# Side work of the tensor engine gathered at parts four and eight of each slot, with the turns priced in the planner (hybrid decoder step, one core)

## The chip, the cores and the metric

The kernel runs on one core of a Trainium2 chip. The metric is the device time of one launch in microseconds (us), on that core; the median of some runs is quoted, and one further execution was recorded by the hardware profiler. A core has a tensor engine (PE, with its weight loads as PEld), a vector engine (DVE), a scalar engine (ACT), GpSimd (POOL), and a queue (SP) that here issues all the transfers between memory and the on-chip buffers.

## The reference

One layer of a decoder is computed for 512 prompt rows and, beside them, for 8 sample rows (one new token in each of 8 sequences with 4096 past tokens, whose keys and values lie in pages of 128 tokens). Everything is fp32.

```python
u = rms_norm(h, g_norm)
z = u @ w_in                                   # 2048 -> 7168
q, k, v, gate_a, cu, gate_c = jnp.split(z, IN_SPLITS, axis=-1)
q, k = partial_rope(q, pos), partial_rope(k, pos)          # 8 heads, two maps of 64 each
o = attn_fn(q, k, v, lam)                      # softmax(map 0) - lam * softmax(map 1), times v
o_att = (rms_norm(o, g_subln) * (1.0 - lam_init)) * jax.nn.silu(gate_a)
g = ca * jax.nn.sigmoid(cb)                    # cu split in two
c = causal_dwconv(hist, w_dw, b_dw)            # 31 taps
o_conv = (jax.nn.silu(layer_norm(c, g_cln, b_cln)) @ w_pw) * jax.nn.silu(gate_c)
h = h + jnp.concatenate([o_att, o_conv], axis=-1) @ w_out
h = h + jax.nn.sigmoid(rms_norm(h, g_ple) @ w_pg) * (p_l @ w_ple)
y = rms_norm(h, g_final)
```

For the prompt, attention is causal over the 512 rows. For the samples it runs over the cache: 8 sequences of 32 key pages and 32 value pages, each page 128 x 1024 numbers (0.524 MB). New keys, values and convolution rows are returned too.

## The kernel before

**Dense products.** All products of the 512 prompt rows with weights are done in 196 slots. A slot loads weights of 256 x 512 (tile `raw`, three buffers); ACT rounds each half to `hi` and POOL takes the rest, `lo = raw - hi`; the activations stand as `aht` and `alt`. Each product is three matmuls of 512 columns into one of four accumulators `acc` (one for each 128 rows of the prompt): hi by high, hi by low, lo by high. A slot has eight parts (four accumulators by two halves of the weights), each part being these three matmuls; the 16 slots of the last two groups of `w_pg` have four parts. There are 4512 such matmuls in the program, and "dense product 3840" below is the 3840th of them. `run_slot` emits the parts and calls `hook(n)` after part n (n from 0).

**Side work.** Everything else that the tensor engine does is put between the parts: transposes through a bank `misc`, the prompt's attention (`att_unit`: scores, transposes of the weights `tmp`, products with `dt`, the transposed result `o`), the statistics of the sample rows, and the decode. The decode has, for each sequence, 32 key pages (tile `kt`, multiplied by the query on DVE, then summed by head on DVE or, sixteen pieces a page, on ACT), a softmax, and 32 value pages (`vt`, or `kt` when the keys are through) that PE multiplies by the weights `aw` into the bank `pers`: four matmuls a page, one on each strip of 32 columns of the array. The sample rows' products with weights are likewise four matmuls on four strips (`pers<-raw,usT`). When the last value page is done, `v_end` and `sample_tail` make the samples' attention output `oS`, multiply it by `w_out` (16 pages of weights through the same two rings, `misc<-kt,mST`), add it to the residual (`xs`), and only then is `usT`, the samples' input to `w_pg`, there; 32 pages of `w_pg` follow (`misc<-kt,usT`). `samp`, in the second slot of the last group, waits for that `usT`.

**What sets the order.** The program is a fixed order for each engine, written when the kernel is built. A class `Planner` keeps a clock for each engine and adds a cost for each instruction it is told of. Each side task is a generator that yields conditions: `on(eng, tiles)` is true when the planned clock of that engine is not ahead of PE's by more than 0.5 us and the tiles are planned to be ready (0.5 us before PE's clock, if PE itself is to read them). `hook` pumps the weight loads and the two rings (five `kt`, two `vt` buffers), resumes each task whose condition holds, and then `decode_tick` gives key products to DVE as long as DVE's planned clock is at most 0.4 us ahead of PE's, and value pages to PE: two or more at any part, a single one only at n = 7. `settle(cond)` is a wait in the plan: it calls `hook` again and again and moves PE's clock until the condition holds, and no dense product is emitted meanwhile. All engines work through their own order and wait for each other by semaphores. All profile rows stand at line 209, the helper that records each instruction, so they are told apart by tiles.

Of the kernel before, what the change touches and what calls it, by code (L numbers as in the profile page):

```python
# [60 lines left out]
class Planner:  # L61
# [2 lines left out]

    FAR = dict(PE=200, V=135, A=130, G=120, Q=70)
    NEAR = dict(PE=0, V=125, A=125, G=60, Q=0)

    def __init__(self):
        self.t = dict(PE=0.0, V=0.0, A=0.0, G=0.0, Q=0.0, D=0.0)
        self.hist = {}  # L70
        self.late = dict(V=[], G=[])

    @staticmethod
    def is_ap(x):
# [86 lines left out]
    def put(self, eng, fn, args, kw, cost=None):  # L161
        outs, ins = [], []
        for i, x in enumerate(args):
            if self.is_ap(x):
                (outs if i == 0 else ins).append(x)
        for k, x in kw.items():
            if self.is_ap(x):
                (outs if k in ("out", "accum_out") else ins).append(x)
        start = self.t[eng]
        dram = lambda x: x.name.startswith(("in_", "out_"))  # L170
        if eng == "Q":
            far = [x for x in outs + ins if dram(x)]
            outs = [x for x in outs if not dram(x)]
            ins = [x for x in ins if not dram(x)]
        start = max([start] + [self.ready(x, True, eng) for x in outs] + [self.ready(x, False, eng) for x in ins])
        if eng == "Q":
            self.t["Q"] = start + 450
            nb = 4
            for d in (outs + ins + far)[0].shape:
                nb *= d  # L180
            self.t["D"] = max(self.t["D"], start + 1100) + nb / 345.0
            end = self.t["D"] + 865
        else:
            c = self.cost(eng, fn, outs, ins, kw) if cost is None else cost
            port = eng in "VG" and self.holds(eng, fn, ins)
            if port:
                start = self.port(eng, start, c)
                self.push(eng, start, c)
            end = start + c
            self.t[eng] = end  # L190
        notes = [self.note(x, True, end, eng) for x in outs] + [self.note(x, False, end, eng) for x in ins]
        if eng in "VG":
            ops = self.late[eng]
            ops.append(dict(at=start, cost=c, port=port, notes=notes))
            del ops[:-16]
# [19 lines left out]
def hymba_step(ctx, tc, x_prompt, x_sample, p_prompt, p_sample, cache_k, cache_v, state_conv, page_table,  # L215
# [4 lines left out]
    plan = Planner()  # L220
    clk = plan.t
# [47 lines left out]
    def on(eng, *aps):  # L269

        back = -500.0 if eng == "PE" else 500.0
        return lambda: (eng == "PE" or clk[eng] <= clk["PE"] + back) and all(plan.ready(x) <= clk["PE"] + back for x in aps)

    def small(n, name, bufs=1):
        return sm.tile([128, n], F32, tag=name, name=name, bufs=bufs)
# [59 lines left out]
    def spawn(gen, now=False, rank=1):  # L335

        tasks.insert(sum(t[2] <= rank for t in tasks), [next(gen) if now else None, gen, rank])

    def hook(n=7):
        wpump()  # L340
        kring.pump()
        vring.pump()
        if cur[0] < 168:
            split_ahead()
        for t in list(tasks):
            for _ in range(3):
                if t[0] is not None and not t[0]():
                    break
                try:
                    t[0] = next(t[1])  # L350
                except StopIteration:
                    tasks.remove(t)
                    break
                if t[0] is None:
                    break
        if cur[0] >= 168:
            split_ahead()
        decode_tick(n)
# [232 lines left out]
    def v_pages(tiled):  # L591

        n = v_here()
        if n < (1 if tiled else 2):
            return
        s = dec["iv"] // NPAGE
        vper[0] = s
        for k in range(n):
            ring = kring if kring.here(VALS) and (not vring.here(VALS) or kring.tiles[0][2] < vring.tiles[0][2]) else vring
            vt, idx = ring.get()  # L600
            for cg in range(4):
                mm(pers[32 * cg:32 * cg + 8, 0:256], aw[s % 2][:, idx % NPAGE, :], vt[:, cg * 256:(cg + 1) * 256],
                   start=False, stop=True, cost=20 if cg else 370 + (0 if k or tiled else 150))
            ring.done(vt)
            dec["iv"] += 1
            vdone[s] += 1
        if vdone[s] == NPAGE:
            spawn(v_end(s), rank=0)
# [236 lines left out]
    def samp(i):  # L845
# [20 lines left out]
        for ii in mem:  # L866
            q = slots[ii]
            for kk in range(2):
                k = q["ks"][kk][0]
                for g in range(4):  # L870
                    mm(pers[32 * g:32 * g + 8, col:col + 128], s["sample"][:, k, :],
                       raws[ii][:, kk, g * 128:(g + 1) * 128], start=False, stop=(q["last"] and kk == 1),
                       cost=20 if g else 214 + 10)
        for ii in mem:
            release(ii)
        if s["last"]:
# [513 lines left out]
    def sample_tail():  # L1390
# [24 lines left out]
        def tail_pass(first, last, lhs):  # L1415
# [3 lines left out]
            for _ in range(last - first):  # L1419
# [5 lines left out]
                for a in range(nn):  # L1425
                    for g in range(4):
                        mm(ps[32 * g:32 * g + 8, (n + a) * 128:(n + a + 1) * 128], lhs[:, k, :],
                           wt[:, a * 512 + g * 128:a * 512 + (g + 1) * 128], start=False, stop=True,
                           cost=20 if g else 214 + 10)
                ring.done(wt)  # L1430
            tail_state["ps"] = ps
        yield from tail_pass(0, 16, mST)
# [42 lines left out]
    with tc.manual_schedule():  # L1475
# [126 lines left out]
        def early_q():  # L1602
# [5 lines left out]
            for n in range(16):  # L1608
# [3 lines left out]
                for a in range(2):  # L1612
                    for g in range(4):
                        mm(pers[32 * g:32 * g + 8, a * 128:(a + 1) * 128], usT[:, k, :],
                           wt[:, a * 512 + g * 128:a * 512 + (g + 1) * 128], start=False, stop=True,
                           cost=20 if g else 214 + 10)
                ring.done(wt)
            yield on("A", pers[:, 0:256])
            qs = yield from take("tmp")
# [103 lines left out]
```

## Time and profile before

| what | value |
|---|---|
| median of 3 runs | 1570.15 us (1565.2 to 1571.04) |
| the profiled execution, its own time | 1576.48 us |
| its span, first to last instruction | 1574.6 us |
| PE / DVE / ACT / POOL busy | 1482.9 / 1100.8 / 811.7 / 622.9 us |
| moved by DMA | 424.40 MB, mean 270 GB/s |
| longest waits of PE, 60 to 1490 us | for `lo` 14.6 us in 26 times, for `pers` 5.0 us in 8 |

The page gives, for each engine, the time in which it was busy; matmuls are pipelined, and the start of one to the start of the next tells better what one costs than its own duration. The view of stretches (windows) gives the same for pieces of the span, with the granted clock of PE (1.00 is 2.4 GHz, 0.50 is 1.2 GHz) and the rate of the transfers. The view in order of time (timeline) lists instructions with their start, their duration, and in brackets the idle time of the engine before them and what ended it.

### The profile page before, as it was taken

The numbers are of one execution on the slowest core, as the hardware profiler recorded it, in microseconds if no ns is written. First come the engines' busy times: TensorE is split into PE (matmuls) and PEld (weight loads), VectorE is DVE, ScalarE is ACT, GpSimd is POOL, SyncE is SP. The second block draws the span as 40 slices with busy tenths as digits, with TensorE's granted clock in tenths as the row PEclk, the third lists the DMA queues.
The fourth block names the chain that finished last, engine by engine and source line by source line (L and its number), as shares of the span: only waits on it lengthen the run. The fifth ranks groups of instructions, "written<-read, shape, count | busy, mean of one in ns | idle before, by whom it ended". The sixth has DMA issues, their size and how long they took to land.

```text
span 1574.6 us, 32145 instructions
## 1 busy us (share of the span) xinstructions
PE 1482.9 (94%) x10448; PEld 1039.5 (66%) x10448; DVE 1100.8 (70%) x1636; ACT 811.7 (52%) x3810; POOL 622.9 (40%) x471
## 2 busy tenths in 40 slices
PE   5899999999999999999999999999999999999786
PEld 4676767666667766677777667766767777665453
DVE  5168987788798978888888868878867888301201
ACT  4156666556655645562445567665655765414202
POOL 5144534323333433344443454434423365425312
PEclk8999999999999999999999999999999999999877
DMA  7648779767887876543358687599878799899997
GB/s 287 233 169 294 273 257 358 275 228 256 320 282 279 296 251 207 188 135 124 126 168 295 228 307 254 187 350 340 299 258 332 275 327 382 306 328 337 395 320 255
DMA packets 148921, 424.40 MB, mean 270 GB/s; under 512 B 14192, under 2 KB 16226, under 8 KB 148480
## 3 DMA queue, kind: packets, MB, share of 16 engines
q1 hardware_dynamic: 148752, 422.35, 75.7%
q8 instruction: 82, 1.34, 0.3%
q14 instruction: 87, 0.71, 0.1%
HBM read 413.62 MB, written 9.63 MB: 269 GB/s over the span
## 4 chain that ended last, share of the span: by engine, by line
PE 75%; DMA 11%; DVE 5%; POOL 3%; issue 3%; ACT 2%; SPq 1%; POOLq 0%; ACTq 0%; DVEq 0%
PE acc L209 57%; PE pers L209 11%; PE misc L209 7%; DMA raw<-in_w_in_dram 4%; POOL lo L209 2%; DVE kt L209 1%; DMA raw<-in_w_out_dram 1%; DMA kt<-in_w_out_dram 1%; DMA raw<-in_w_pg_dram 1%; DVE bt L209 1%; DMA vt<-in_cache_v_dram 1%; DVE sc L209 1%; DMA kt<-in_w_pg_dram 1%; DMA kt<-in_cache_v_dram 0%; ACT hi L209 0%
## 5 line engine op out<-in xcount | busy, mean ns | idle before, releaser
L209 POOL TENSOR_TENSOR lo<-raw,hi 128x512 fp32r<-128x512 f32 x392 | 557.7, 1435 | 829.7 <-ACT hi L209 775.1
L209 ACT CAST hi<-raw 128x512 fp32r<-128x512 f32 x392 | 236.6, 618 | 437.1 <-PE acc L209 218.1
L209 DVE TENSOR_TENSOR kt<-kt,qb 128x1024 f32<-128x1024 f32 x256 | 363.9, 1436 | 41.1 <-DMA kt<-in_cache_k_dram 36.7
L209 PE MATMUL acc<-hi,aht 128*128 128x512 f32 x896 | 377.8, 422 | 7.8 <-ACT hi L209 7.5
L209 PE MATMUL acc<-lo,aht 128*128 128x512 f32 x896 | 360.9, 403 | 17.5 <-POOL lo L209 17.5
L209 PE MATMUL acc<-hi,alt 128*128 128x512 f32 x896 | 357.9, 399 | 0.2 <-DVE alt L209 0.2
L209 ACT ACTIVATE kt<-kt 128x64 f32<-128x64 f32 x1392 | 336.1, 244 | 25.2 <-DVE kt L209 25.2
L209 ACT ACTIVATION_READ_ACCUMULATOR kt<-kt 128x1 f32 x1392 | 262.2, 188 | 0.0
L209 PE MATMUL acc<-aht,hi 128*128 128x512 f32 x576 | 245.6, 426 | 3.9 <-DVE bt L209 3.4
L209 PE MATMUL acc<-aht,lo 128*128 128x512 f32 x576 | 228.8, 397 | 4.5 <-POOL lo L209 4.4
L209 PEld LDWEIGHTS acc<-hi,aht 128*128 128x128 f32 x896 | 170.2, 190 | 92.8 <-issue 32.4
L209 PE MATMUL acc<-alt,hi 128*128 128x512 f32 x576 | 227.5, 395 | 0.0
L209 PEld LDWEIGHTS acc<-lo,aht 128*128 128x128 f32 x896 | 170.7, 190 | 68.4 <-POOL lo L209 28.3
L209 DVE TENSOR_REDUCE sc<-kt 128x16 f32<-128x1024 f32 x169 | 203.4, 1210 | 1.3
L209 PEld LDWEIGHTS acc<-hi,alt 128*128 128x128 f32 x896 | 171.2, 191 | 33.3 <-DVE alt L209 0.7
L209 DVE SCALAR_TENSOR_TENSOR misc<-ft,wdwT,misc 128x512 f32<-128x512 f32 x240 | 180.3, 751 | 6.2
L209 PEld LDWEIGHTS acc<-aht,hi 128*128 128x128 f32 x576 | 108.5, 188 | 65.0 <-issue 34.3
L209 PEld LDWEIGHTS acc<-aht,lo 128*128 128x128 f32 x576 | 108.2, 188 | 34.8 <-POOL lo L209 9.2
L209 PEld LDWEIGHTS acc<-alt,hi 128*128 128x128 f32 x576 | 108.6, 189 | 18.0 <-issue 0.2
L209 PE MATMUL pers<-vt,aw 128*8 128x256 f32 x1624 | 113.4, 380 | 6.3 <-DVE pers L209 5.0
L209 DVE SCALAR_TENSOR_TENSOR acc<-acc,ct 128x512 f32<-128x512 f32 x16 | 11.2, 699 | 128.9 <-ACT acc L209 128.9
L209 PEld LDWEIGHTS pers<-vt,aw 128*8 128x8 f32 x1624 | 31.8, 88 | 62.9 <-issue 32.5
(259 smaller groups left out, 1283.2 us busy)
## 6 DMA issues: line engine op xcount, KB each, us to landing
kt<-in_cache_k_dram SPq DMA_DIRECT2D x256, 512.0 KB
vt<-in_cache_v_dram SPq DMA_DIRECT2D x203, 512.0 KB
raw<-in_w_in_dram SPq DMA_DIRECT2D x112, 512.0 KB
kt<-in_cache_v_dram SPq DMA_DIRECT2D x53, 512.0 KB
raw<-in_w_pg_dram SPq DMA_DIRECT2D x40, 512.0 KB
raw<-in_w_out_dram SPq DMA_DIRECT2D x32, 512.0 KB
kt<-in_w_in_dram SPq DMA_DIRECT2D x12, 512.0 KB
kt<-in_w_out_dram SPq DMA_DIRECT2D x12, 512.0 KB
```

The source lines that it names most:

```text
L209: real(*args, **kw)
```

## The change

The planner gets a constant `TURN = 92` (ns): whenever PE goes from a dense product to anything else, or back, 92 ns are added to the planned cost. The other planned costs of strip matmuls are set anew: a value page 410 + 3 x 7 ns for its four matmuls (before: 370 + 3 x 20, and 150 more for the first page of a run at another part than the last), a set of four sample matmuls 205 + 3 x 7 (before 224 + 3 x 20). And a condition is added: tasks that wait with `on("PE", ...)`, and value pages, may go on only when `turn()` holds, that is, after part 4 and part 8 of a slot (n = 3 and 7), or while no dense product runs, or in a `settle`. Tasks that wait for a free bank alone (`take`), or for a page in a ring, are not held back. No instruction is computed otherwise; the order and the place of the side work change, and with the planned clock the place of the work on the other engines.

```diff
     FAR = dict(PE=200, V=135, A=130, G=120, Q=70)
     NEAR = dict(PE=0, V=125, A=125, G=60, Q=0)
+    TURN = 92
...
             c = self.cost(eng, fn, outs, ins, kw) if cost is None else cost
+            if eng == "PE":
+
+                dense = outs[0].name.startswith("acc")
+                c += self.TURN if dense != self.dense else 0
+                self.dense = dense
...
-        return lambda: (eng == "PE" or clk[eng] <= clk["PE"] + back) and all(plan.ready(x) <= clk["PE"] + back for x in aps)
+        return lambda: (eng != "PE" or turn()) and (eng == "PE" or clk[eng] <= clk["PE"] + back) and all(plan.ready(x) <= clk["PE"] + back for x in aps)
...
+    step = [0]
+
+    def turn():
+
+        return not main_on[0] or step[0] % TURNS == TURNS - 1
+
+    TURNS = 4
+
     def hook(n=7):
+        step[0] = n
         wpump()
...
         n = v_here()
-        if n < (1 if tiled else 2):
+        if n < (1 if tiled else 2) or not turn():
             return
...
-                   start=False, stop=True, cost=20 if cg else 370 + (0 if k or tiled else 150))
+                   start=False, stop=True, cost=7 if cg else 410)
...
-                       cost=20 if g else 214 + 10)
+                       cost=7 if g else 205)
```

The last pair of lines stands at three more places (`samp`, `tail_pass`, `early_q`).

In the built program both kernels have the same 7697 matmuls. What changes is where they stand. On PE, in the first half of the prompt's attention, these rows follow each other before (`misc<-ft,bt` are scores, `misc<-cst,tmp` and `misc<-cst,o` transposes, `misc<-dt,tmp` products with the values, `pers<-vt,aw` value pages of the decode, four matmuls each):

```order
L209 MATMUL misc<-cst,o 128x128
L209 MATMUL acc<-aht,hi 128x512
L209 MATMUL acc<-alt,hi 128x512
L209 MATMUL acc<-aht,lo 128x512
L209 MATMUL misc<-cst,tmp 128x128
L209 MATMUL pers<-vt,aw_121 8x256 x8
L209 MATMUL acc<-aht,hi 128x512
L209 MATMUL acc<-alt,hi 128x512
L209 MATMUL acc<-aht,lo 128x512
L209 MATMUL misc<-dt,tmp 128x128
L209 MATMUL misc<-ft,bt 128x384 x2
```

And now, in the same half of the attention:

```order
L216 MATMUL misc<-cst,o 128x128
L216 MATMUL misc<-dt,tmp 128x128 x4
L216 MATMUL pers<-vt,aw_120 8x256 x8
L216 MATMUL acc<-aht,hi 128x512
L216 MATMUL acc<-alt,hi 128x512
L216 MATMUL acc<-aht,lo 128x512
L216 MATMUL acc<-aht,hi 128x512
L216 MATMUL acc<-alt,hi 128x512
L216 MATMUL acc<-aht,lo 128x512
```

Side work that stood after single parts of three products now stands together, with two to four parts in a row between. Over the whole program the runs of side work go from 387 to 321; the changes of the array's tile shape (128x128, four strips of 32 columns, or row tiles) from one matmul to the next go from 573 to 549.

On PE near the end, before, from the last value pages to the first dense product after them (`misc<-tmp,cst` and `misc<-cst,oS` belong to the attention output of the samples, `misc<-kt,mST` and `misc<-vt,mST` are the pages of `w_out`, `misc<-cst,xs` the new residual, `pers<-raw,usT` the sample product that needs it):

```order
L209 MATMUL pers<-kt,aw_121 8x256 x8
L209 MATMUL misc<-tmp,cst 128x128 x4
L209 MATMUL misc<-cst,oS 128x128 x2
L209 MATMUL misc<-kt,mST 8x128 x32
L209 MATMUL misc<-vt,mST 8x128 x16
L209 MATMUL misc<-kt,mST 8x128 x40
L209 MATMUL misc<-vt,mST 8x128 x16
L209 MATMUL misc<-kt,mST 8x128 x24
L209 MATMUL misc<-cst,xs 128x128 x4
L209 MATMUL misc<-stat,cst 128x1
L209 MATMUL pers<-raw,usT 8x128 x16
L209 MATMUL acc<-hi,aht 128x512
```

And the same pages of `w_out` now, of which these are the first seven:

```order
L216 MATMUL misc<-kt,mST 8x128 x8
L216 MATMUL acc<-hi,aht 128x512
L216 MATMUL acc<-hi,alt 128x512
L216 MATMUL acc<-lo,aht 128x512
L216 MATMUL misc<-kt,mST 8x128 x24
L216 MATMUL acc<-hi,aht 128x512
L216 MATMUL acc<-hi,alt 128x512
L216 MATMUL acc<-lo,aht 128x512
L216 MATMUL misc<-kt,mST 8x128 x8
L216 MATMUL misc<-vt,mST 8x128 x8
L216 MATMUL misc<-kt,mST 8x128 x8
```

Before, the last value page, all of `w_out` for the samples and the new residual stand in one piece at dense product 4440, in the `settle` of `samp`; now the last value page stands at 4284, `w_out` between 4356 and 4398, and the residual at 4404, all between dense products. The decode's place along the dense products, as the order has it:

| done by dense product | key products before / now | value pages before / now |
|---|---|---|
| 1536 | 108 / 105 | 74 / 63 |
| 2304 | 131 / 139 | 96 / 108 |
| 2880 | 158 / 169 | 128 / 138 |
| 3840 | 237 / 251 | 172 / 186 |

Of the key pages 87 are summed on ACT before and 98 now, the others on DVE (169 and 158). The last multiplication by the row factor in the convolution's layer norm, which the first slot of `w_pw` at dense product 2880 needs, stands at dense product 2850 before and at 2880 now, with a `settle` in front of that slot.

## Rows read from the trace of the kernel before

**Rows 1.** The page, part 1: busy us, share of the span, instructions.

```profile
PE 1482.9 (94%) x10448; PEld 1039.5 (66%) x10448; DVE 1100.8 (70%) x1636; ACT 811.7 (52%) x3810; POOL 622.9 (40%) x471
```

**Rows 2.** Stretches: length; busy PE, PEld, DVE, ACT, POOL (instructions); clock, DMA share, GB/s.

```profile
560.00:810.00 250.00, 243.20 (x1657) 174.81 (x1661) 207.42 (x398) 120.64 (x503) 96.84 (x80) 1.00 0.50 169
1280.00:1482.00 202.00, 197.41 (x1336) 127.34 (x1338) 76.19 (x94) 83.86 (x293) 98.63 (x75) 1.00 0.93 342
1482.00:1519.00 37.00, 22.21 (x329) 13.10 (x322) 6.18 (x19) 1.42 (x6) 1.94 (x3) 0.61 0.95 357
1519.00:1562.00 43.00, 39.37 (x552) 25.30 (x552) 3.00 (x7) 8.36 (x16) 12.52 (x10) 0.90 0.89 296
1562.00:1575.00 13.00, 0.59 (x2) 0.50 (x2) 4.84 (x11) 4.51 (x10) 1.88 (x3) 0.64 0.46 166
```

**Rows 3.** PE in order of time at the end: start, us, what, [idle before].

```profile
1480.17 0.39 PE L209 MATMUL acc<-lo,aht 128*128 128x512 f32 x1
...
1485.12 0.62 PE L209 MATMUL pers<-kt,aw 128*8 128x256 f32 x8 [2.72 <-DMA kt<-in_cache_v_dram]
...
1493.20 0.69 PE L209 MATMUL misc<-cst,oS 128*128 128x128 f32 x2 [3.57 <-DVE oS L209]
1494.84 3.60 PE L209 MATMUL misc<-kt,mST 128*8 128x128 f32 x64 [0.95 <-PE misc L209]
...
1505.26 1.04 PE L209 MATMUL misc<-kt,mST 128*8 128x128 f32 x16 [2.16 <-DMA kt<-in_w_out_dram]
...
1516.94 1.89 PE L209 MATMUL pers<-raw,usT 128*8 128x128 f32 x32 [0.16 <-DVE usT L209]
1518.76 0.80 PE L209 MATMUL acc<-hi,aht 128*128 128x512 f32 x1
...
1560.80 1.06 PE L209 MATMUL misc<-kt,usT 128*8 128x128 f32 x32
```

**Rows 4.** PE in order of time: one transpose among dense products.

```profile
401.25 0.39 PE L209 MATMUL acc<-aht,lo 128*128 128x512 f32 x1
401.48 0.27 PE L209 MATMUL misc<-cst,o 128*128 128x128 f32 x1
...
401.83 0.39 PE L209 MATMUL acc<-alt,hi 128*128 128x512 f32 x1
```

**Rows 5.** The same view: one value page, then four transposes, among dense products.

```profile
644.96 0.40 PE L209 MATMUL acc<-aht,lo 128*128 128x512 f32 x1
645.29 0.62 PE L209 MATMUL pers<-vt,aw 128*8 128x256 f32 x8
...
646.17 0.40 PE L209 MATMUL acc<-alt,hi 128*128 128x512 f32 x1
646.40 0.39 PE L209 MATMUL acc<-aht,lo 128*128 128x512 f32 x1
646.64 0.60 PE L209 MATMUL misc<-cst,tmp 128*128 128x128 f32 x4
...
647.30 0.40 PE L209 MATMUL acc<-alt,hi 128*128 128x512 f32 x1
```

**Rows 6.** The same view: two value pages among dense products.

```profile
460.84 0.40 PE L209 MATMUL acc<-lo,aht 128*128 128x512 f32 x1
461.17 1.05 PE L209 MATMUL pers<-vt,aw 128*8 128x256 f32 x16
...
462.48 0.39 PE L209 MATMUL acc<-hi,alt 128*128 128x512 f32 x1
```

**Rows 7.** The same view: the first slot of `w_pw`.

```profile
990.06 0.50 PE L209 MATMUL acc<-aht,hi 128*128 128x512 f32 x1 [2.54 <-DVE bt L209]
```

**Rows 8.** The page, part 5 (groups): a key product, part of a sum.

```profile
L209 DVE TENSOR_TENSOR kt<-kt,qb 128x1024 f32<-128x1024 f32 x256 | 363.9, 1436 | 41.1 <-DMA kt<-in_cache_k_dram 36.7
...
L209 ACT ACTIVATE kt<-kt 128x64 f32<-128x64 f32 x1392 | 336.1, 244 | 25.2 <-DVE kt L209 25.2
...
L209 DVE TENSOR_REDUCE sc<-kt 128x16 f32<-128x1024 f32 x169 | 203.4, 1210 | 1.3
```

More of the change, by code (lines that the diff above doesn't have):

```diff
@@ L71, in __init__ @@
         self.late = dict(V=[], G=[])
+        self.dense = False
     @staticmethod
@@ L1428, in tail_pass @@
                            wt[:, a * 512 + g * 128:a * 512 + (g + 1) * 128], start=False, stop=True,
-                           cost=20 if g else 214 + 10)
+                           cost=7 if g else 205)
                 ring.done(wt)
@@ L1615, in early_q @@
                            wt[:, a * 512 + g * 128:a * 512 + (g + 1) * 128], start=False, stop=True,
-                           cost=20 if g else 214 + 10)
+                           cost=7 if g else 205)
                 ring.done(wt)
```

## The prediction

> **What bounds the kernel now.** I read the page first, then the stretches, then PE in order of time. PE is busy for 94% of the span [rows 1], so two things can shorten the time: PE work that goes away, or stretches in which PE has nothing dense to do. The stretches show where these are. From 560 to 810 us PE is busy for 243 of 250 us at full clock, while the transfers run at 169 GB/s; from 1280 to 1482 us it is still full, and the transfers run at 342 GB/s with a share of 0.93; from 1482 to 1519 us PE is busy for 22 of 37 us, at a granted clock of 0.61, partly its 1.2 GHz level [rows 2]. The order of time tells why: the last dense product before the hole starts at 1480.17, the next at 1518.76. Between them stand the last value pages (one waits 2.72 us for its transfer), the samples' attention output (PE waits 3.57 us for DVE), the samples' product with `w_out`, whose pages come by DMA, and at last `pers<-raw,usT`, the product for which the plan had stopped [rows 3]. So the run has two programs side by side, dense products and decode, and the decode arrives late: for 38.6 us the dense products wait for its end. Before that, PE bounds; in the hole, the decode's chain and its transfers do.
>
> **The change, part by part.** Sums are made against the profiled execution, 1576.48 us with a span of 1574.6; the median of the runs, 1570.15, is 0.996 of that, and I scale by this at the end.
>
> *Turns on PE.* A dense product that follows another takes 0.23 us (401.25 to 401.48). One transpose between two dense products moves the second one after it from 0.46 to 0.58 us, by 0.12 [rows 4]; four of them move it from 0.46 to 0.90, by 0.11 each [rows 5]. Side work on the whole array therefore pays nothing for its turn. One value page makes 1.21 of 0.46 us [rows 5], two make 1.64 [rows 6]: 0.43 for a page and 0.32 for going to the four strips and back, 0.16 for each change of shape. The order has 573 such changes before and 549 now: 24 x 0.16 = 3.8 us less. The 66 runs of side work that go away otherwise give nothing. The Trainium skill has a rule here (TensorEngine Tiling (Array Packing), Tiling Modes, Key Properties): changing the tiling mode, not just the tile, drains the engine. The rows agree, and so the rule speaks against the planner's new constant, which charges every turn alike: by the constant's idea, 66 runs fewer at the strips' 0.32 us would be 21 us; by rule and rows it is the 3.8 us. The new page and sample costs change no instruction, only the plan.
>
> *The hole at the end.* In the new order the last value page stands at dense product 4284 instead of 4440, `w_out` for the samples at 4356 to 4398, and the new residual at 4404, 36 dense products before the product that waits for it. The decode is ahead because in the second half of the prompt's attention the plan's PE clock runs slower (two turns for each run of side work), and so lets DVE do more key products for each dense product: by 2304 there are 139 for 131, by 3840 251 for 237, with 186 value pages for 172. What goes is the part of the hole that isn't PE work. Dense start to dense start it is 38.59 us [rows 3], less the 0.23 of one product: 38.4. PE work in it at full clock: six value pages, 2.6; 32 sets of four sample matmuls for `w_out`, half a page's columns each, 0.22, so 6.9; four sets for `usT`, 0.9; the transposes and the four products for the attention output, 14 records of about 0.11, 1.6; three goings to the strips and back, 1.0. That is 13.0, and 25.4 us go. That they don't come back is bounded by the 36 dense products: with 0.23 us each and the work between them they cover over 8 us, where the way from the residual to `usT` is short (the sample product waited 0.16 us for `usT` [rows 3]).
>
> *The clock after it.* From 1519 to 1562 the granted clock is 0.90 [rows 2]. At 1.00 throughout, at most 0.10 x 43 = 4.3 us would go; part of it belongs to later waits for transfers that stay. I take 1.
>
> *The layer norm.* Side chains now wait for part four or eight before each step on PE, and the last multiplication of the layer norm slips from dense product 2850 to 2880, just in front of the first slot that needs it. That slot waits 2.54 us already [rows 7], so nothing is left to hide the slip: 30 products x 0.23 = 6.9 us at most, nothing at least. I take 4. All of PE's queue stands behind that wait.
>
> *DVE and ACT in the middle.* Between dense products 1536 and 2304, which take from 554 to 810 us when the records are counted along the trace, there are now 34 key products instead of 23. On DVE that is 11 x 1.436 = 15.8 us, on ACT, which takes 18 sums instead of 7, 11 x 16 x 0.244 = 42.9 us [rows 8]. The stretch leaves DVE 42.6 us idle and ACT 129 us [rows 2]. It fits, but the idle time of DVE is partly time in which it waits for attention results, so some of the dense products' casts and banks will come later: between 0 and 15.8, and I take 3, near the lower end since the idle time is over twice the addition. There are also 45 value pages in it instead of 22. The 34 pages more are 34 x 0.524 = 17.8 MB, 71 GB/s on top of 169 [rows 2], well under the 342 that the end shows.
>
> *Transfers at the end.* From 1280 (dense product 3840 stands at 1282) to 1562 us, 342 x 202 + 357 x 37 + 296 x 43 = 95.0 MB are moved [rows 2]. The 28 pages done earlier take 14.7 MB from that; 80.3 MB at 342 GB/s are 235 us. PE has 282 - 25.4 - 6.0 (14 value pages done earlier) = 250 us for it. So transfers stay under PE by 15 us; at the 296 GB/s of the last stretch they would take 271 and cost 21. I take 2.
>
> **Sum:** -25.4 - 3.8 - 1 + 4 + 3 + 2 = -21.2, so 1555.3 us for the profiled execution and, by 0.996, 1549 for the median. What is late next is the same decode chain after the last pages of `w_pg`, from 1562 to the end [rows 2, 3], which the change leaves as it is.
>
> **The rivals.**
> *No new wait* (0.11): the three costs are zero and the clock gives its 4.3: -33.5, 1543 for the execution, 1537 for the median. For it: PE's idle time in 560 to 810 is under 7 us of 250 already at 83% DVE [rows 2]. Against it: the layer norm's row.
> *The transfers bound the end* (0.12): the decode is ahead in the order, but the last 80 MB come at the rate of the last stretch, and the hole is spread over many short waits for pages: -30.2 + 7 + 21 = -2, so 1574 and 1568, no change that shows. For it: the share of 0.93 before the hole and of 0.95 in it [rows 2]. Against: 342 and 357 GB/s were held there, and less is asked for.
> *The other engines become the bound* (0.07), the case that ends slower. The plan counts 73 runs of side work that stay on the whole array with 0.184 us too much each, 13.4 us in which PE is faster than the plan and the other engines are not. From dense product 1536 to 3840 DVE gets 146 key products instead of 129 and 87 sums instead of 84: 17 x 1.436 + 3 x 1.210 = 28.0 us [rows 8]. With the layer norm's 6.9 that is 48.3; if all of it lands on PE: +18, 1595 and 1588. It is slower by over 0.5% only if more than 38 of the 48 land there. Against: DVE has 42.6 us idle in the first 250 us of that stretch alone [rows 2].
>
> **How the numbers follow.** The forecast, the hole gone and small waits new, gets 0.70. Its own range is 1540 to 1562: from costs near zero to about 20 us of them. Half a per cent, about what a measurement of this kernel can tell from no change, is 7.9 us, so faster means under 1562.3: forecast and first rival, 0.81; the second rival is the same, 0.12; the third slower, 0.07. The range that should hold 8 times in 10 goes from 1536 (every cost zero, the clock back) to 1565, where the costs reach 25 (7, 8 and 10); left out are the third rival, half of the second and a little below.
>
> **What would show it.** In the profile after: no stretch of over 10 us without dense products before the last 15 us, and a granted clock of 1.00 where 1482 to 1519 stood; transfers well above 169 GB/s between dense products 1536 and 2304; PE busy less by about 4 us, besides what the slow clock had added; a wait of some 4 to 9 us at the first slot of `w_pw`; the chain after the last `w_pg` page still about 13 us. I am wrong if the dense products still stop for `usT`, if waits for `vt` and `kt` transfers from dense product 3840 on come to over 20 us, or if PE's waits for DVE and ACT in the attention grow to tens of us.

## The result, and the profile after

The changed kernel takes 1542.67 us (median of 4 runs, 1537.34 to 1546.48) beside 1567.68 for the kernel before (4 runs on the same chip): a ratio of 0.984, 95% interval 0.9818 to 0.9861. It is faster by 25 us; forecast were 1549 and a range of 1536 to 1565. The profiled execution took 1543.31 us with a span of 1541.5, against 1576.48 and 1574.6.

First the page, part 1, of the changed kernel, which answers to [rows 1]:

```profile
PE 1464.2 (95%) x10448; PEld 1037.8 (67%) x10448; DVE 1089.7 (71%) x1625; ACT 852.6 (55%) x4162; POOL 627.3 (41%) x471
```

PE executes the same 10448 matmuls and is busy for 18.7 us less. The stretches say where that comes from. They answer to [rows 2]; the first runs from dense product 1536 to 2304, which is where the 250 us of before lay, the others cover the end (columns: length; busy PE, PEld, DVE, ACT, POOL; granted clock; DMA share; GB/s):

```profile
532.00:802.00 270.00, 262.27 (x1892) 184.07 (x1881) 229.30 (x424) 155.61 (x781) 100.47 (x81) 1.00 0.66 227
...
1482.00:1519.00 37.00, 32.16 (x426) 20.65 (x425) 0.64 (x2) 6.84 (x12) 16.54 (x15) 1.00 0.84 282
...
1526.00:1541.00 15.00, 3.28 (x74) 1.75 (x65) 6.25 (x15) 5.65 (x13) 1.87 (x3) 0.71 0.57 199
```

In the middle the transfers run at 227 GB/s instead of 169, and DVE stands idle for 41 of 270 us (43 of 250 before): the decode is done earlier, as the order had it. At the end the clock is 1.00 where it was 0.61. The hole itself, in PE's order of time, against [rows 3]:

```profile
1469.30 0.60 PE L216 MATMUL misc<-cst,xs 128*128 128x128 f32 x4
...
1485.01 0.39 PE L216 MATMUL acc<-lo,aht 128*128 128x512 f32 x1
1485.33 1.06 PE L216 MATMUL pers<-raw,usT 128*8 128x128 f32 x32
1486.32 0.50 PE L216 MATMUL acc<-hi,aht 128*128 128x512 f32 x1
```

Dense product 4440 is at 1485.01 and the next at 1486.32: 1.31 us where it was 38.59. The residual `xs` is transposed 16 us earlier, and `pers<-raw,usT` waits for nothing. The longest way between two dense products is now 5.8 us, at 45 us, long before the end.

To compare whole executions, I divide the time of each trace from the first dense product to the last, record of PE by record. 4511 dense products at the usual 0.2334 us from start to start are 1052.9 us in each kernel. Idle time of PE is counted by what stands behind it, a dense product or side work. "Slow clock" is PE's busy time multiplied by what the granted clock lacks to 1.00. What is left is the side work with its turns; being a remainder, it also takes up what the other columns miss. "Ends" is the time ahead of the first dense product and behind the start of the last. The changes of shape are counted in the order of PE, as in the prediction. The columns from the side work on add up, with the 1052.9 us, to the span of the profiled execution, some 1.8 us under its time in the third column, and not to the median: the profiled execution of the kernel before took 8.8 us more than its median, so the two traces differ by 33.1 us and the medians by 25.0.

| kernel | median us | profiled us | changes of shape | side work and turns | idle before dense | idle before side work | slow clock | ends |
|---|---|---|---|---|---|---|---|---|
| before | 1567.7 | 1576.5 | 573 | 397.7 | 32.3 | 36.4 | 25.0 | 30.4 |
| changed | 1542.7 | 1543.3 | 549 | 392.8 | 27.4 | 27.3 | 9.3 | 31.9 |
| e1 gate alone | 1549.8 | 1548.8 | 530 | 390.3 | 19.8 | 37.9 | 15.6 | 30.5 |
| e2 costs alone | 1566.9 | 1569.3 | 608 | 412.0 | 30.7 | 27.8 | 12.7 | 31.4 |
| e3 before, decode ahead | 1554.6 | 1557.5 | 573 | 397.9 | 30.0 | 27.3 | 12.2 | 35.4 |
| e4 changed, decode behind | 1543.8 | 1544.2 | 536 | 389.7 | 16.1 | 37.8 | 15.3 | 30.6 |
| e5 points two and six | 1542.2 | 1547.9 | 589 | 401.3 | 29.5 | 17.2 | 13.5 | 31.7 |
| e6 gate, decode ahead | 1548.7 | 1554.2 | 550 | 391.7 | 24.7 | 32.9 | 20.1 | 30.3 |
| e7 one point, hole kept | 1567.2 | 1567.9 | 492 | 382.7 | 27.9 | 46.2 | 26.0 | 30.5 |
| e8 one point, first half | 1555.5 | 1559.4 | 538 | 387.3 | 30.8 | 31.3 | 18.7 | 36.8 |
| e9 pages after the zeroing | 1529.4 | 1529.5 | 555 | 389.9 | 19.6 | 19.5 | 9.6 | 36.2 |
| e10 the same, hole kept | 1540.5 | 1540.3 | 547 | 390.0 | 19.8 | 26.1 | 19.3 | 30.4 |
| e11 as e9, 2.5 us | 1529.0 | 1526.4 | 566 | 391.5 | 23.4 | 12.8 | 8.1 | 36.1 |
| e12 as e9, 0.8 us | 1537.5 | 1535.4 | 566 | 395.5 | 25.7 | 17.6 | 5.6 | 36.3 |

From before to changed the side work loses 4.9 us, the two kinds of idle time 14.0 and the slow clock 15.7. Most of it is one place: from dense product 4416 to the last one the idle time falls by 10.2 (19.8 to 9.6) and the slow clock by 13.8 (13.8 to 0.0). Ahead of that, side work now waits more (25.5 against 21.1) and dense products less (19.5 against 27.9). The rows of PE's waits from 60 to 1480 us show for what (us in total, times, longest); the table ahead of the prediction has 14.6 in 26 for `lo` and 5.0 in 8 for `pers` before:

```profile
PE pers L216 <- DVE pers L216: 10.1, 13, 2.8
PE acc L216 <- POOL lo L216: 8.4, 19, 0.9
PE pers L216 <- DMA vt<-in_cache_v_dram: 4.4, 7, 1.5
...
PE acc L216 <- ACT aht L216: 3.4, 1, 3.4
PE acc L216 <- ACT hi L216: 3.3, 4, 1.4
```

The first row is new in size, and the experiments come back to it.

### The profile page after: what moved, and what is told of

It reads as the page before. It is cut to its first block, busy times and chain, and to the rows that moved or that the text cites. A ratio compares the mean times of both kernels' runs of the same rounds, so it can differ in the third digit from the quotient of the medians.

```text
span 1541.5 us, 32434 instructions
## 1 busy us (share of the span) xinstructions
PE 1464.2 (95%) x10448; PEld 1037.8 (67%) x10448; DVE 1089.7 (71%) x1625; ACT 852.6 (55%) x4162; POOL 627.3 (41%) x471
## 4 chain that ended last, share of the span: by engine, by line
PE 73%; DMA 12%; DVE 6%; POOL 3%; ACT 2%; issue 2%; SPq 1%; POOLq 0%; ACTq 0%; DVEq 0%
PE acc L216 55%; PE pers L216 11%; PE misc L216 6%; DMA raw<-in_w_in_dram 4%; POOL lo L216 3%; DMA vt<-in_cache_v_dram 3%; DVE kt L216 2%; DMA raw<-in_w_out_dram 1%; DMA kt<-in_cache_k_dram 1%; DMA kt<-in_w_pg_dram 1%; SPq L216 1%; DVE sc L216 1%; ACT hi L216 1%; DVE bt L216 1%; DMA raw<-in_w_pg_dram 1%
## 5 line engine op out<-in xcount | busy, mean ns | idle before, releaser
L216 ACT ACTIVATE kt<-kt 128x64 f32<-128x64 f32 x1568 | 378.5, 244 | 18.0 <-DVE kt L216 18.0
L216 DVE TENSOR_TENSOR kt<-kt,qb 128x1024 f32<-128x1024 f32 x256 | 352.8, 1391 | 38.7 <-DMA kt<-in_cache_k_dram 35.3
L216 PE MATMUL acc<-lo,aht 128*128 128x512 f32 x896 | 359.9, 402 | 14.4 <-POOL lo L216 14.3
L216 ACT ACTIVATION_READ_ACCUMULATOR kt<-kt 128x1 f32 x1568 | 296.3, 189 | 0.0
L216 PE MATMUL acc<-aht,hi 128*128 128x512 f32 x576 | 242.4, 421 | 4.2 <-ACT aht L216 3.4
L216 PEld LDWEIGHTS acc<-lo,aht 128*128 128x128 f32 x896 | 169.7, 189 | 65.8 <-POOL lo L216 26.1
L216 DVE TENSOR_REDUCE sc<-kt 128x16 f32<-128x1024 f32 x158 | 189.8, 1209 | 1.3
L216 PEld LDWEIGHTS acc<-aht,lo 128*128 128x128 f32 x576 | 108.7, 189 | 31.7 <-POOL lo L216 5.8
L216 PE MATMUL pers<-vt,aw 128*8 128x256 f32 x1656 | 114.1, 380 | 13.9 <-DVE pers L216 9.4
L216 DVE SCALAR_TENSOR_TENSOR acc<-acc,ct 128x512 f32<-128x512 f32 x16 | 11.2, 700 | 128.2 <-ACT acc L216 128.1
```

What stands on the lines that cost most here:

```text
L216: real(*args, **kw)
```

## The experiments

**One part alone.** The change has two parts: the gate (`turn()` in the conditions), and the prices (`TURN` and the strip costs). e1 keeps the gate and takes the old prices, e2 the other way round.

```diff
 # e1, against the changed kernel (the other strip costs likewise)
-    TURN = 92
+    TURN = 0
-                   start=False, stop=True, cost=7 if cg else 410)
+                   start=False, stop=True, cost=20 if cg else 370 + (0 if k or tiled else 150))
 # e2, against the changed kernel
-        return lambda: (eng != "PE" or turn()) and (eng == "PE" or clk[eng] ...
+        return lambda: (eng == "PE" or clk[eng] ...
-        if n < (1 if tiled else 2) or not turn():
+        if n < (1 if tiled else 2):
```

> The gate of the change alone: PE-side tasks and value pages wait for parts four and eight, but the planned costs are those of before (no turn priced, old page and sample costs). In the built order the runs of side work are 299 (before 387, changed kernel 321), the changes of tile shape 530 (573, 549), and the last value page, the samples' w_out and the residual stand at dense product 4440 again, in the settle. Theory (the decode's place against the dense products decides, the gathering gives 0.16 us a shape change): 43 changes fewer, -7, and up to 4 of new waits, so 1560 to 1567 us, with the hole of about 38 us at the end as before. Rival (gathering the side work is what shortens the time): as fast as the changed kernel or faster, 1536 to 1545.

> The planned costs of the change alone: 92 ns for each turn and the new page and sample costs, without the gate. In the built order the shape changes are 608 (before 573), the runs of side work 408 (387), the last value page stands at dense product 4119 and the residual at 4215, and no settle stands at 4440. Theory: the hole goes, -25, and 35 shape changes more cost 6, so 1545 to 1552 us, with no dense products missing for more than 10 us before the last stretch. Rival (gathering): nothing is gathered, so no faster than before, 1567 to 1575.

e1 took 1549.84 us (ratio 0.9895, 0.9862 to 0.9928), e2 1566.87 (1.000, 0.9983 to 1.0017). e2 came out where its rival had it; e1 lies between its theory and its rival. So the prices put the decode ahead: with them the hole is gone (the longest way between two dense products in e2 is 6.1 us), without them it stays (45.9 us in e1). But they alone bring nothing, since their order has 35 changes of shape more than before, and side work that is 14.3 us longer. The gate alone brings 18 of the 25 us with the hole in full: its idle time before dense products falls by 12.5, its slow clock by 9.4 and its side work by 7.4.

**The hole alone.** The limit by which DVE's planned clock may run ahead when a key product is given to it is another handle on the decode. e3 raises it in the kernel before, which removes the hole there; e4 lowers it in the changed kernel, which brings the hole back.

```diff
 # both places in decode_tick; e3 in the kernel before, e4 (200) in the changed kernel
-            elif more and clk["V"] <= now + 400:
+            elif more and clk["V"] <= now + 550:
```

> The kernel before with two numbers changed: key products and their sums may be given to DVE while its planned clock is up to 0.55 us ahead of PE's, instead of 0.4. No gate, no turn price, old costs. Built order: 573 shape changes, as before, 396 runs of side work, the last value page at dense product 4320, the residual at 4404, no settle at 4440. Theory: the hole goes by this alone, 1540 to 1550 us. Rival (gathering, or the turn prices as such): no change, 1563 to 1571.

> The changed kernel with the same two numbers at 0.2 us instead of 0.4, so that the decode falls behind again while the gate and the prices stay. Built order: 536 shape changes, 305 runs of side work, the last value page, w_out and the residual all at dense product 4440, with the settle. Theory: the hole returns, +25, 13 shape changes fewer give 2, so 1560 to 1570 us. Rival (gathering): 1535 to 1545.

e3 took 1554.63 us (0.9911, 0.988 to 0.9941), e4 1543.75 (0.9851, 0.9815 to 0.9887). Here e3 lies between its theory and its rival, and e4 is where its rival had it. Without the hole the kernel before gains 13.6 us, about half of the 25.4 that the forecast gave for it; by the two traces 23.4 us of idle time and slow clock go behind dense product 4416, and 5.1 come back in the ends. With the hole the changed kernel loses nothing that can be measured. e4's hole is real, 33 us with PE at 0.62 of its clock:

```profile
1454.00:1487.00 33.00, 20.06 (x314) 11.71 (x312) 8.13 (x23) 3.98 (x10) 3.54 (x5) 0.62 0.85 308
```

The table says what pays for it: e4 has 11.3 us less idle time before dense products than the changed kernel and 3.1 us less side work. Its order is freer elsewhere: it has 13 changes of shape fewer, and no wait for `aht` at `w_pw`.

**Where the gate's two points stand.** The first of my new theories was that side work after part eight stands ahead of the next slot's first dense product, and covers the casts (`hi`, `lo`) that this product waits for. e5 moves the points; e6 gives e1 the decode ahead.

```diff
 # e5, against the changed kernel (decode_tick and the waiting hook follow)
-        return not main_on[0] or step[0] % TURNS == TURNS - 1
+        return not main_on[0] or step[0] % TURNS == 1
 # e6: e1 with the limit 550 of e3
```

> The changed kernel with the two points moved: side work on PE may go after parts two and six of each eight, not after four and eight. 589 changes of shape on PE instead of 549, 356 runs of side work instead of 321; the end is free of the hole in both. Theory (side work after part eight stands in front of the first dense product of the next slot and covers the casts that this product waits for): 1542.7 + 40 x 0.16 = 1549.1 for the turns, plus about 8 for the cover that is gone, 1557; the dense products' idle time at part one of a slot, from 60 us to dense product 4416, goes back from 8.9 (with the 3.4 of one wait at `w_pw`) to 12 or more, where the kernel before has 15.0. Rival (two points are enough, wherever they stand): 1549, and the idle time at part one stays under 9.

> The gate alone, with the old costs and no price on turns as in e1_gate_alone, and the decode sent ahead by another way: DVE's key products are taken when its plan is up to 0.55 us ahead, not 0.4. The hole of e1 at dense product 4440 is gone; 550 changes of shape instead of 530. Theory (the hole's worth is kept in part only, since the waits for pages and casts that it had hidden come back): the hole's idle time, 10.6 us, and its slow clock, 6.3, go; 20 x 0.16 = 3.2 for the turns and up to 7.6 in waits before dense products come back: 1549.8 - 16.9 + 3.2 + 7.6 = 1544. First rival (the hole is worth its 24.8 us in each kernel): 1549.8 - 24.8 + 3.2 = 1528. Second rival (with the gate the hole is worth nothing): 1553.

e5 took 1542.22 us (0.9842, 0.9817 to 0.9867), e6 1548.66 (0.9875, 0.9848 to 0.9902). e5 refutes the theory as it stood: the idle time at part one is 11.2 us, more than 8.9 but under the 12, and the time is neither the 1557 of the theory nor the 1549 of the rival, but that of the changed kernel. Its turns are dearer as expected (401.3 - 392.8 = 8.5 for 40 changes, 0.21 each), but 10.1 us of idle time before side work are gone. Its rows of PE's waits, 60 to 1440 us, show which:

```profile
PE acc L216 <- POOL lo L216: 10.7, 24, 1.3
PE pers L216 <- DMA vt<-in_cache_v_dram: 4.9, 5, 1.7
PE acc L216 <- ACT hi L216: 2.1, 4, 1.1
```

No wait of `pers` for DVE's work on that bank (`PE pers <- DVE pers`) is left. e6 lies between its theory (1544) and its second rival (1553). Its waits of that kind are twice those of e1 (first e1, then e6, 60 to 1480 us):

```profile
PE pers L216 <- DVE pers L216: 8.4, 12, 1.0
PE pers L216 <- DVE pers L216: 16.4, 16, 2.9
```

By the two traces e6 has 24.1 us less idle time and slow clock than e1 behind dense product 4416 and 28.3 more ahead of it: 13.9 of slow clock and 14.4 of idle time, 8.0 of which are those waits. That is the trace of an execution 5.6 us over e6's median, so how much of the slow clock the other executions have is not known.

**One point in eight parts.** If turns were what counts, fewer would be better.

```diff
 # e7 (e8: 128 in place of 232); both with the limit 550
-        return not main_on[0] or step[0] % TURNS == TURNS - 1
+        t = 8 if dec["iv"] < 232 else TURNS
+        return not main_on[0] or step[0] % t == t - 1
```

> The changed kernel with one point in each eight parts instead of two until 232 of the 256 value pages are done, two from there on, and DVE's limit 0.55 us. The hole at the end stands as in e4_behind_again, so the two compare: 492 changes of shape instead of 536, 248 runs of side work instead of 305, but the layer norm's last step stands in front of the first slot of `w_pw`. Theory (a change of shape costs 0.16 us, a run on the whole array nothing): 1543.8 - 44 x 0.16 = 1536.8, plus about 3 at `w_pw`: 1540. First rival (each run pays for its two turns, 0.32): 1543.8 - 57 x 0.32 + 3 = 1529. Second rival (the turns are worth nothing where the gate already gathers): 1547.

> The changed kernel with one point in each eight parts until 128 of the 256 value pages are done, two from there on, and DVE's limit 0.55 us. No hole at the end; 538 changes of shape instead of 549, 274 runs instead of 321, and in the first half all side work after part eight. Theory: 1542.7 - 11 x 0.16 = 1540.9, less about 2 for casts covered in the first half: 1539. Rival (as much is lost in the first half where single chains wait longer for their point): 1543 or more.

e7 took 1567.24 us (0.9999, 0.9982 to 1.0016), e8 1555.45 (0.9927, 0.9902 to 0.9952). Both are misses, by 27 and 16 us; e8 is where its rival had it (1543 or more). The turns did what the theory says: e7's side work is 7.0 us under e4's, 44 changes at 0.16, although it has 57 runs fewer. All that was gained there is lost in waits, which were in none of the three forecasts of e7; how much of them the limit of 550 brings, which e4 does not have, was not tried apart (PE's waits, 60 to 1440 us):

```profile
PE acc L216 <- POOL lo L216: 11.6, 18, 1.8
PE pers L216 <- DMA vt<-in_cache_v_dram: 11.2, 11, 5.0
PE pers L216 <- DVE pers L216: 11.0, 13, 2.9
PE misc L216 <- DVE mx L216: 5.4, 2, 3.1
```

At one point a slot the value pages stand in longer runs, and they wait for their transfers. One place, in PE's order of time and as a stretch:

```profile
993.03 1.04 PE L216 MATMUL pers<-vt,aw 128*8 128x256 f32 x8 [5.01 <-DMA vt<-in_cache_v_dram]
...
996.53 0.80 PE L216 MATMUL acc<-aht,hi 128*128 128x512 f32 x1 [1.22 <-ACT aht L216]
```

```profile
992.60:1003.00 10.40, 8.55 (x31) 5.04 (x31) 10.40 (x15) 8.46 (x38) 0.25 (x1) 0.51 0.60 213
```

A wait of 5 us is followed by 10 us at 0.51, where a dense product goes from 0.23 to 0.43 us from start to start. Each of the eleven stretches at slow clock in e7's trace begins during or shortly after a wait of PE of 0.9 us or more, while about as many such waits are followed by full clock (2.37 us at 956, for one). I therefore read the slow clock (26.0 in all) as a price that some waits have, not as a thing of its own.

**The waits for `pers`.** e5 and e7 point to the row that the change had doubled. The changed kernel's trace shows what such a wait is, first PE, then DVE, in order of time:

```profile
1185.51 1.06 PE L216 MATMUL pers<-raw,mST 128*8 128x128 f32 x32
1189.35 1.05 PE L216 MATMUL pers<-vt,aw 128*8 128x256 f32 x16 [2.79 <-DVE pers L216]
```

```profile
1187.03 1.21 DVE L216 TENSOR_TENSOR kt<-kt,qb 128x1024 f32<-128x1024 f32 x1
1188.16 0.67 DVE L216 TENSOR_TENSOR bt<-bt,acc 128x512 f32<-128x512 f32 x1
1188.76 0.27 DVE L216 TENSOR_TENSOR xs<-pers,xs 128x128 f32<-128x128 f32 x1
1189.13 0.17 DVE L216 MEMSET pers<- 128x128 f32 x1
```

`pers` is one bank: columns 0 to 255 hold the sum of the value pages, 256 to 511 those of the samples' products. When a group of slots ends, its samples' product is read and its part of the bank zeroed by DVE or, for the reading, ACT. A value page that stands behind that product in PE's order waits until the zeroing is done, though it writes other columns. The planner asks only whether the weights and the page are ready, so it doesn't see this. In all 13 cases the page starts some 0.05 us after the memory set of the samples' 128 columns has ended. Ten of the waits are of 0.65 to 0.68 us; the long one is this, with a key product and other work of DVE in front: 2.79. The samples' product stands behind part eight, and the gate sends the value pages to the same point; after parts two and six (e5) they don't meet. That the wait can't simply be left out is in line with the Trainium skill (PSUM — Partial Sum Buffer, PSUM bank collisions raise a hardware error), which asks for semaphores by bank and quadrant, not by address; no run here tried two engines in one bank.

e9 therefore keeps the wait and moves the page:

```diff
 # e9, in v_pages of the changed kernel; e11 with -2500, e12 with -800
         if n < (1 if tiled else 2) or not turn():
             return
+        if plan.ready(pers, True) > clk["PE"] + -1500:
+            return
 # e10: e9, and in v_here
-                if kind != VALS or idx // NPAGE != s or plan.ready(t) > clk["PE"]:
+                if kind != VALS or idx // NPAGE != s or plan.ready(t) > clk["PE"] - 300:
```

> The changed kernel, where a value page goes into PE's queue only when the plan has the bank `pers` zeroed 1.5 us before. In the changed kernel's trace value pages wait 10.1 us for DVE at `pers` (13 waits; the longest, 2.79 us at 1189, is followed by 3.4 us at half the clock, 1.7 us of work). 555 changes of shape instead of 549; the end is free of the hole, and the layer norm's last step isn't in front of `w_pw` any more (wait 3.4 us, and a slow stretch at 979 to 986 behind the pages there, about 3.4). Theory (what is left over the pure work is waits of PE and the slow clock behind the longest of them; dense products stand in their place now): 1542.7 - 8 - 1.7 - 6.8 + 6 x 0.2 = 1527. Rival (the wait moves: pages that come later come in longer runs, and wait for their transfers or make others late): 1539 to 1545.

> As e9_pages_after_zeroing, and a value page also goes into the queue only 0.3 us after the plan has it in the chip's memory. By this the decode falls behind, and the hole at the end is back as in e4_behind_again: 547 changes of shape against 536 there. Theory: the waits of value pages for DVE at `pers`, 9.8 us in e4, and for `vt`, 1.4, go but for 2, 11 x 0.2 for the turns come: 1543.8 - 9 + 2.2 = 1537, with 20 us or more idle in front of side work behind dense product 4416. Rival (the wait moves): 1544 or more.

e9 took 1529.38 us (0.9741, 0.9712 to 0.9769), e10 1540.53 (0.9805, 0.9771 to 0.9839). e9 beats both kernels, by 40 us and by 13 (by the ratios to the kernel before, 0.9741 against 0.984, the intervals are well apart). All PE's waits of over 1.6 us in total between 60 and 1480 us are these five; `pers` for DVE isn't among its rows at all, nor the wait for `aht` at `w_pw`:

```profile
PE acc L216 <- POOL lo L216: 7.5, 18, 0.6
PE misc L216 <- DVE tmp L216: 5.4, 4, 2.9
PE acc L216 <- ACT hi L216: 3.8, 3, 1.3
PE misc L216 <- DMA kt<-in_w_out_dram: 3.0, 1, 3.0
PE misc L216 <- ACT tmp L216: 2.4, 5, 1.2
```

Not all of the 13 us is the bank: the wait at `w_pw`, 3.39 us, and 2.5 us for the slow clock in and behind it went too, because the layer norm's last step moved.

e10, with the hole back, is 3.5 us over its forecast and 11 over e9. From dense product 4416 to the last it has 8.7 us more idle time (14.9 against 6.2) and 7.8 more slow clock (9.4 against 1.6), and 5.8 less in its ends, together 10.7, by which the two traces differ. So here, where the rest of the two orders comes to the same, the hole is worth what its rows say, which e4 had hidden. An order has its own luck, so e11 and e12 make other orders by the same rule:

> As e9_pages_after_zeroing with 2.5 us between the plan's zeroing of `pers` and a value page, not 1.5: another order with the same effect on the waits. 566 changes of shape instead of 555, no hole at the end. Theory (the waits for the zeroing are what e9 took away): no value page waits for DVE at `pers`, and 1529.4 + 11 x 0.2 = 1531.6. Rival (e9 is a lucky order, and another one with the same rule falls back to the changed kernel): 1540 or more.

> As e9_pages_after_zeroing with 0.8 us between the plan's zeroing of `pers` and a value page, not 1.5. 566 changes of shape instead of 555, no hole at the end. Theory: most waits for the zeroing in the changed kernel are of 0.65 us, so 0.8 takes those away and leaves the few long ones, where DVE is later than the plan has it: 1529.4 + 11 x 0.2 + up to 3 + 1.7 behind a long one = 1532 to 1536. Rival (lucky order): 1540 or more.

e11 took 1528.99 us (0.9764, 0.9735 to 0.9793) and has no wait for DVE at `pers` either; e12 took 1537.54 (0.9815, 0.9788 to 0.9842), 1.5 over its range. In e12 those waits are down to 0.19 us, less than I had expected, but its side work is 5.6 us longer than e9's and its dense products wait 6.1 us longer. Orders that differ by a small step of one number thus differ by some 8 us with the same waits for `pers`; e9's gain of 13 is more than that, e12's of 5 is not, and what e12 lost I did not follow further.

## Why the prediction was right, and where it was not

**The hole, right.** -25.4 and -1 for the clock; from dense product 4416 on the idle time and the slow clock together fell by 24.0. Its cause was right as well: the prices put the decode ahead (e2, against e1). That they do so by `TURN` rather than by the strip costs was not tried apart.

**The turns, right.** -3.8; measured -4.9 in the side work. e4 to e7 gives 0.16 us for a change of shape, the changed kernel to e5 0.21, a line through all kernels of the table but e2 0.18. The step that runs on the whole array pay nothing for their turn holds in PE's work: e7 has 57 runs fewer than e4 and 7.0 us less side work, what 44 changes account for, not the 18 of a price for each run. e2's side work is some 9 us above that line, and what it consists of stays open.

**The layer norm, right in size.** +4; the wait at the first slot of `w_pw` is 3.39 us instead of the 2.54 of [rows 7], below the 4 to 9 that I named as its sign, but the stretch from 979 to 986, which begins in that wait, is granted 0.51, and its 5.12 us of PE work cost 0.49 x 5.12 = 2.5 more, 3.4 with the wait's 0.85:

```profile
976.87 0.62 PE L216 MATMUL pers<-vt,aw 128*8 128x256 f32 x8 [0.25 <-DMA vt<-in_cache_v_dram]
980.88 0.79 PE L216 MATMUL acc<-aht,hi 128*128 128x512 f32 x1 [3.39 <-ACT aht L216]
```

```profile
979.00:986.00 7.00, 5.12 (x11) 3.80 (x12) 7.00 (x12) 5.26 (x13) 0.00 (x0) 0.51 0.51 183
```

**DVE in the middle, and the transfers: the size within the bounds, the place wrong.** I took 3 and 2 for work that comes later on DVE and in the queue. Casts came no later; the new costs are the 5.1 us of waits for `pers`, the slow clock behind the longest of them (0.53 from 1190.8 to 1194.4), and waits for transfers, from 60 us to dense product 4416 6.8 us instead of 1.4, of which 4.4 are for value pages well ahead of the end:

```profile
1190.80:1194.40 3.60, 3.60 (x11) 2.81 (x10) 3.60 (x4) 0.62 (x1) 1.96 (x1) 0.53 0.99 352
```

The step that failed is the one on the gate: I asked who is late when a task waits for its point, and not what it then stands behind on PE. At part eight that is the samples' product and the zeroing of its bank.

**What the sum left out.** The forecast is 6 us too slow against the median and 12 against the profiled execution (1555.3 and 1543.3), on which the sum was made. That the miss of the median is the smaller is luck: the profiled execution of the kernel before lay high, and the factor 0.996 takes off half of the miss. Ahead of dense product 4416, where the sum has 9 us of new waits, idle time and slow clock fell by 5.8 in the traces. The sum is too slow because it gives the gate nothing but its turns ("The 66 runs of side work that go away otherwise give nothing"). As a statement on time that step was wrong: e1 has its hole in full and still gains 18 us, and by its trace, which lies 27.7 us under that of before, side work with 43 changes of shape fewer is 7.4 of it, shorter waits before dense products 12.5 and the slow clock 9.4. From 60 to 1480 us PE waits 6.2 us less for `lo` in the changed kernel than before. That side work in front of a slot covers these casts explains a part at most: from 60 us to dense product 4416 the idle time at part one of a slot is 15.0 us before and 8.9 in the changed kernel, but 11.2 in e5, whose side work stands after parts two and six, and e5 is no slower. Why e1 and e4 have as little idle time before dense products (19.8 and 16.1) as e9 and e10 isn't settled.

**The terms don't add.** The sum treats the hole and the gate as separate gains. One by one they give 13.6 (e3) and 18 (e1), together 25, and the hole brought back costs nothing in e4. The forecast came out because it followed one order, from its own rows, and because what it left out stayed within its range; its terms would not hold in another order.

**The signs** that I had named: no stretch of over 10 us without dense products before the last 15, seen; clock 1.00 in place of the hole, seen; transfers well above 169 GB/s in the middle, seen (227); PE busy less by 4 us beside the slow clock, seen (18.7 less 15.7 is 3.0); the wait at `w_pw`, just below; a last chain of some 13 us, seen (the last page ends at 1529.95, and 11.6 us follow; before 12.7):

```profile
1528.89 1.06 PE L216 MATMUL misc<-kt,usT 128*8 128x128 f32 x24 [0.86 <-DMA kt<-in_w_pg_dram]
```

Of the rivals, none came. There are new waits (`pers`, `aht`), so the first is out as it stood, though by the time alone its 1537 is as near as the 1549. The transfers didn't bind: from dense product 3840 (1275 us) to the end PE's waits for them come to 5.2 us, not to over 20.

```profile
PE misc L216 <- DMA kt<-in_w_pg_dram: 2.8, 5, 0.9
PE misc L216 <- DMA kt<-in_w_out_dram: 2.4, 3, 1.1
```

DVE and ACT didn't either: PE's waits for them from 60 us to dense product 4416 are 22.7 us, against 23.1 before.

## What to carry to other kernels

When side work on an engine is gathered at few points, ask what it stands behind at those points: a task that comes together with another may inherit its wait, here by a shared bank that the planner looked at only in part. Fewer turns are worth what rows show for a turn (0.16 to 0.21 us here) and no more; with one point a slot, waits for inputs lose more than that (e7). And a change that only reorders should be judged by the whole account of one order, since gains that are each measured alone do not add.

## What the runs showed of the hardware

Short waits of PE had a second price. In the changed kernel 2.79 us of waiting for the zeroing are followed, 1.4 us after it, by 3.6 us at a clock of 0.53, partly the 1.2 GHz level, some 1.7 us of lost work; in e7 5.01 us by 10.4 at 0.51. It is not a rule that every such wait brings this on: the wait of 2.54 us in [rows 7] was followed by full clock (1.00 from 990 to 994). And going to the strips and back costs 0.32 us by [rows 5] and [rows 6], beside 0.43 for each page, while transposes on the whole array cost 0.11 to 0.12 each and nothing for the turn. The count of such changes in the order is thus nearly enough to know PE's own work: the line of 0.18 us for each meets the side work of thirteen of the fourteen kernels to within 3.5 us. It was fitted to them afterwards, and e2 lies 9 us above it.
